# Key and value projection of a two-layer decoder: six slabs and eight plain quads per group, a new order of their jobs, squares by pairs of chunks

## The chip, the cores and the metric

The kernel runs on one core of a Trainium2 chip. The metric is device time in microseconds (us) of one execution of the whole program, as the median of several runs. All data are float32. Where the text says PE, DVE, ACT, POOL and SP it means TensorE, VectorE, ScalarE, GpSimd and SyncE.

## The reference, cut to what matters

Two layers work on a stream of 256 tokens of width 2048. Layer 0 is a pooling mixer beside a memory attention, then an MLP. From the stream after layer 0 the keys and values are made once. Layer 1 is a differential attention over them, a memory attention and an MLP. The change lies in `shared_kv` and around it:

```
def shared_kv(x, kv_norm, w_kv, k_norm, cos, sin):
    B, S, _ = x.shape
    kv = rms_norm(x, kv_norm) @ w_kv
    k1 = kv[..., :DIFF_QK_WIDTH].reshape(B, S, DIFF_HEADS, DIFF_HEAD_DIM)
    k2 = kv[..., DIFF_QK_WIDTH:2 * DIFF_QK_WIDTH].reshape(B, S, DIFF_HEADS, DIFF_HEAD_DIM)
    v = kv[..., 2 * DIFF_QK_WIDTH:].reshape(B, S, DIFF_HEADS, DIFF_V_DIM)
    k1 = partial_rope(rms_norm(k1, k_norm), cos, sin)
    k2 = partial_rope(rms_norm(k2, k_norm), cos, sin)
    return k1, k2, v
```

`w_kv` is 2048 x 3072: 768 columns of `k1`, 768 of `k2` and 1536 of `v`. The mean square of each token, which `rms_norm` needs, is applied after the product, as a factor per token.

## The kernel before, in words

**Three matmuls for one product.** Every weight is split into a part `hi`, rounded by an ACT cast (L195), and a part `lo`, the rest, by a DVE subtraction (L198). The activations are split in the same way. A product of 128 rows of weights is then three matmuls: low activations by `hi`, high by `hi`, high by `lo` (L1650 to L1652). The split weights stand in a ring of six slots of 512 columns (`hi_ring`, `lo_ring`). A job takes one or two neighbouring slots, a slot is free again when the job's matmuls are done, and `AHEAD` is three: splits of up to three later jobs are put into the program ahead of a job's matmuls. So for a slot the chain is: last matmul on it, cast, subtraction, next matmul.

**Quads and slabs.** The 3072 columns of `w_kv` are done as a last block of 512 columns of keys (tile `k1`), a last block of values (tile `v1`, the steps H), and two groups of 1024 columns, one of values (`vp`) and one of keys (`kp`). In a group the work comes in two shapes. A plain quad is one 128-row chunk of the stream by 512 columns, for both halves of the tokens: two products, six matmuls, one slot, loaded with another quad in one DMA of SP into a `raw` tile. A slab is two chunks by 1024 columns by the two halves of the tokens in seven products in place of eight: two by two blocks, with sums of blocks of the stream (`kv_sums`, made on DVE and ACT ahead) and sums of blocks of weights. Its job 0 is two products on one side of the weights and takes two slots, job 1 is one product and one slot, jobs 2 and 3 are two products and two slots each: 21 matmuls where four plain quads have 24. The sums of weights are made while the weights come in: the left half of a slab is loaded by SP (L158), job 0 splits it, then POOL adds the right half to it by an accumulating DMA (`add_right`, L170), and job 1 can be split only after that DMA has landed. In the same way POOL's second accumulating DMA stands between the splits of job 2 and of job 3. Two DVE additions per slab (L224, L238) make the other sums. Left halves stand in three buffers (tag `rows`), second ones in three (`feed.second`).

**The order of the jobs** is written by hand in the string `steps` (L1726): a pair of digits is a slab and its job (slabs 0 to 4 of values, 5 to 9 of keys), H a step of `v1`, A and B plain quads of values, C and D of keys, M a step of the memory values of layer 1 (tile `mv`), which the loop at L1870 makes, E and X, Y copies and closings. `close` (L1654) adds a group's seven banks up on DVE and ACT once the group's last slab is through. A scheduler then orders what the program says on each engine, so the queues differ a little from the program text.

**Other work of the same stretch** is hung on a counter that goes up with every step: `at(d, fn)` runs `fn` at the d-th step from now. Under way are the squares of the stream for its mean square (`later_square`, L752), the second load and split of the memory (`mem_again`, `mem_split`, tile `mems`), the sums of the stream's blocks (`kv_sums`, L1594), and at the end the normalisation of the keys and the scaled stream of layer 1 (`x_mx`). `two_squares` (L1334) exists already: it squares two chunks with one ACT instruction into the one buffer of tag `rowsq` and adds them on DVE to a sum of 512 columns; the last call adds the two halves.

Of the kernel before, what the change touches and what calls it, by code (L numbers as in the profile page):

```python
# [10 lines left out]
F32 = mybir.dt.float32  # L11
F32R = mybir.dt.float32r
AF = mybir.ActivationFunctionType
# [4 lines left out]
P = 128  # L18
T = 256
NK = 16  # L20
# [291 lines left out]
def program(ctx, tc, plan, dry, xT, memT, par, lam, cst, wst, yT):  # L312
    nc = tc.nc
# [3 lines left out]
    tp = ctx.enter_context(tc.tile_pool(name="tp", bufs=1))  # L317
# [5 lines left out]
    acc = {}  # L323
# [18 lines left out]
    def vt(name):  # L342
        return tp.tile([P, T], F32, tag="v", bufs=6, name=name)
# [13 lines left out]
    resid = cp.tile([P, NK, T], F32, name="resid")  # L357
# [40 lines left out]
    def gcol(c):  # L398
        return param[:, c : c + 1]
# [342 lines left out]
    def add_square(key, src, first):  # L742
# [5 lines left out]
        sq = vt("psq")  # L748
        nc.scalar.activation(sq, src, AF.Square)
        nc.vector.tensor_add(acc[key], acc[key], sq)  # L750

    def later_square(n):  # L752

        if n == 0:
            acc["x"] = tp.tile([P, T], F32, tag="acc", bufs=1, name="acc")
            nc.scalar.activation(acc["x"], resid[:, 0, :], AF.Square)
            return
        sq = vt("later")
        nc.scalar.activation(sq, resid[:, n, :], AF.Square)
        nc.vector.tensor_add(acc["x"], acc["x"], sq)  # L760

    def resid_add(ps, n):
        nc.vector.tensor_add(resid[:, n, :], resid[:, n, :], ps[:, 0:T])
# [784 lines left out]
    x_kv = sp.tile([P, NK, 512], F32R, tag="S2", name="x_kv")  # L1548
    x_in.append(x_kv)
    down()  # L1550
    for n in range(NK):
        at(2 + n // 2, lambda n=n: later_square(n))
    kv = sp.tile([P, 4096], F32, tag="big", name="kv1")
    kv2 = sp.tile([P, 2048], F32, tag="big2", name="vv1")
    kT = kv[:, 0:3072].rearrange("p (c t) -> p c t", c=12)
# [7 lines left out]
    def mem_again(p):  # L1563
        t = kv[:, p % 3 * 512 : p % 3 * 512 + 512].rearrange("p (k t) -> p k t", k=2)
        nc.sync.dma_start(t, memT[:, 2 * p : 2 * p + 2, :])

    def mem_split(k):
        t = kv[:, k % 6 * T : k % 6 * T + T]
        split_gain(mems1[:, k, :], t, gcol(G_MEM + 16 + k))

    for p in range(8):
        at(5 * p + 3 if p >= 3 else 4 + p // 2, lambda p=p: mem_again(p))
    for k in range(NK):
        at(12 + 9 * k // 4, lambda k=k: mem_split(k))

    ktab = rope_tables(G_KR, "krope")
    qtab = rope_tables(G_QR, "qrope")
# [16 lines left out]
    def kv_sums(i):  # L1594

        a = [vt("kv_a") for _ in range(2)]
        for e in range(2):
            k = 2 * i + e
            nc.scalar.activation(a[e], resid[:, k, :], AF.Copy, scale=gcol(G_KV + k))
        hi, lo = sums[:, i, 0:512], sums[:, i, 512:1024]  # L1600
        f = kv[:, 1536:2048]
        s1, s2, s3, s4 = (f[:, c * P : c * P + P] for c in range(4))
        (a11, a21), (a12, a22) = ((x[:, 0:P], x[:, P:T]) for x in a)
        if i >= 5:
            nc.vector.tensor_sub(s1, a11, a21)
            nc.vector.tensor_sub(s2, a12, a22)
            hi, lo, f = hi[:, 0:T], lo[:, 0:T], f[:, 0:T]
        else:
            nc.vector.tensor_sub(s1, a21, a22)
            nc.vector.tensor_sub(s3, a11, a21)  # L1610
            nc.vector.tensor_sub(s2, s1, a11)
            nc.vector.tensor_add(s4, a12, s2)

        def split():
            nc.scalar.copy(hi, f)
            nc.vector.tensor_sub(lo, f, hi.bitcast(F32))

        at(1, split)

    for i, d in enumerate((16, 23, 30, 38, 48, 42, 45, 52)):  # L1620
        at(d, lambda i=i: kv_sums(i))

    c1 = []
# [5 lines left out]
    def kv_groups():  # L1629
# [51 lines left out]
        slab = {}  # L1681

        def job(n, j):
            g, i = divmod(n, 5)
            if j == 0:
                slab[n] = feed.slab(
                    [blocks_of(g, 2 * i, c) + blocks_of(g, 2 * i + 1, c) for c in range(2)]
                )

            def plain(c, t):  # L1690
                x = x_kv[:, 2 * i + c, :]
                return x[:, t * P : t * P + P], x[:, T + t * P : T + t * P + P]

            def summed(c):
                return tuple(sums[:, i, b + c * P : b + c * P + P] for b in (0, 512))

            sides = (
                ((0, lambda: plain(0, 0)), (1, lambda: plain(1, 0))),
                ((2, lambda: summed(0)),),
                ((3, lambda: summed(1)), (4, lambda: summed(3))),  # L1700
                ((6, lambda: plain(1, 1)), (5, lambda: summed(2))),
            )
            hi, lo = feed.job(slab[n], j)
            for c, (p, a) in enumerate(sides[j]):
                s = slice(512 * c, 512 * c + 512)
                product(g, p, a(), hi[:, s], lo[:, s])
            feed.job_used(slab[n], j)
            tick()
            if i == 4:
                close(g, j)  # L1710

        def plain_quad(g, c, k):
            what = blocks_of(g, k, c)
            hi, lo = feed.quad(what if len(what) > 1 else what[0])
            x = [(x_kv[:, k, t * P : t * P + P], x_kv[:, k, T + t * P : T + t * P + P]) for t in range(2)]
            if c:
# [7 lines left out]
        last_v = []  # L1724
        ps = [pp.tile([P, 512], F32, tag=g, bufs=1, name="v1") for g in "ot"]
        steps = """  # L1726
            H H H H
            00 H H H H
            10 H 01 H 02 H H
            20 H 11 H H H E 12 30 03  # L1730
            A 21 A 22 A 13 A
            40 B 31 B 32 B 23 B
            B B 41 A 42 A 33 X 50
            C 43 C 60 C C 51 52
            D 70 C 61 62 C 53
            D 80 D 71 72 D 63
            90 D 81 D 82 Y 73 M M
            M 91 M 92 M 83 M
            M M 93
        """.split()  # L1740
        last_of = {}
        for n, x in enumerate(steps):
            if x in "ABCD":
                g, bs = dict(A=(0, (1, 6)), B=(0, (4, 2)), C=(1, (4, 2)), D=(1, (1, 6)))[x]
            elif x[0].isdigit():
                g, bs = int(x[0]) // 5, ((0, 1), (2,), (3, 4), (5, 6))[int(x[1])]
            else:
                continue
            for p in bs:
                last_of[g, p] = n  # L1750
        now_at = [-1]
        count = dict.fromkeys("HABCD", 0)
        values = dict(A=(0, 0), B=(0, 1), C=(1, 1), D=(1, 0))

        def more():

            while steps:
                x = steps.pop(0)
                now_at[0] += 1
                n = count.get(x, 0)  # L1760
                if x in count:
                    count[x] += 1
                if x == "M":
                    return True
                if x == "H":
                    wide_step(ps, ("w_kv", 0, n, 5, 4), x_kv, n)
                elif x == "E":
                    for t in range(2):
                        last_v.append(tp.tile([P, 512], F32, tag=("acc2", "rowsq")[t], bufs=1, name="v_c"))
                        nc.scalar.activation(last_v[t], ps[t], AF.Copy, scale=c1[0][:, t : t + 1])  # L1770
                elif x in "XY":
                    close("XY".index(x), 4)
                elif x in values:
                    plain_quad(*values[x], 10 + n)
                else:
                    job(int(x[0]), int(x[1]))
            return False

        def end():
# [364 lines left out]
```

## Time and profile before

| | |
|---|---|
| runs before | 1983.72, 1983.87, 1984.21 us, median 1983.87 us |
| the profiled execution | 1983.49 us |
| its span, first to last instruction | 1981.5 us |
| granted clock of PE | 1.00 throughout |
| PE, DVE, ACT busy share of the span | 100%, 91%, 79% |
| the stretch of the change | about 880 to 1110 us from the span's start: `k1` at 920 to 942, `v1` and `vp` to 1007, `kp` to 1055, then the rest of `mv` and the memory keys |

The profile is of one execution. Its own time is 2.0 us longer than its span and 0.38 us below the median of the runs. Busy time counts the stretches in which an engine has an instruction under way. Matmuls overlap each other, so a PE that is busy all the time is not yet shown to be free of waiting: there the starts of the matmuls have to be read.

### The profile page before, as it was taken

The numbers are of one execution on the slowest core, as the hardware profiler recorded it, in microseconds if no ns is written. First come the engines' busy times: TensorE is split into PE (matmuls) and PEld (weight loads), VectorE is DVE, ScalarE is ACT, GpSimd is POOL, SyncE is SP. The second block draws the span as 40 slices with busy tenths as digits, with TensorE's granted clock in tenths as the row PEclk, the third lists the DMA queues.
The fourth block names the chain that finished last, engine by engine and source line by source line (L and its number), as shares of the span: only waits on it lengthen the run. The fifth ranks groups of instructions, "written<-read, shape, count | busy, mean of one in ns | idle before, by whom it ended". The sixth has DMA issues, their size and how long they took to land.

```text
span 1981.5 us, 31968 instructions
## 1 busy us (share of the span) xinstructions
PE 1977.1 (100%) x10356; PEld 1685.5 (85%) x10356; DVE 1806.3 (91%) x3320; ACT 1569.6 (79%) x2894; POOL 238.7 (12%) x281
## 2 busy tenths in 40 slices
PE   9999999999999999999999999999999999999999
PEld 8888888888888888888888889888888888888888
DVE  8888889999999999889989798989999999999888
ACT  7766677788878888778868699777788888888775
POOL 0000011111111111110110000001111111111110
PEclk9999999999999999999999999999999999999999
DMA  9556578888888898766885534568888888888764
GB/s 316 181 184 198 187 203 233 237 228 235 237 232 233 228 235 227 226 183 228 244 223 191 162 126 145 195 188 242 234 230 230 234 234 228 242 231 231 229 203 146
DMA packets 151080, 426.92 MB, mean 215 GB/s; under 512 B 17024, under 2 KB 19712, under 8 KB 150912
## 3 DMA queue, kind: packets, MB, share of 16 engines
q1 hardware_dynamic: 111024, 352.50, 53.3%
q0 software_dynamic: 39744, 72.37, 21.9%
q8 instruction: 81, 1.33, 0.3%
q14 instruction: 87, 0.71, 0.1%
q10 hardware_dynamic: 144, 0.01, 0.0%
HBM read 422.72 MB, written 2.10 MB: 214 GB/s over the span
## 4 chain that ended last, share of the span: by engine, by line
PE 99%; DMA 0%; SPq 0%; ACT 0%; issue 0%; DVE 0%
PE x_bank L456 22%; PE x_bank L458 11%; PE p L953 10%; PE p L955 10%; PE p L956 10%; PE wo L456 6%; PE wo L458 3%; PE u L456 2%; PE ff L456 1%; PE u L458 1%; PE q L490 1%; PE q L492 1%; PE q L491 1%; PE mk L492 1%; PE mk L490 1%; PE mk L491 1%
## 5 line engine op out<-in xcount | busy, mean ns | idle before, releaser
L195 ACT CAST hi_ring<-raw 128x512 fp32r<-128x512 f32 x897 | 546.7, 619 | 169.4 <-PE x_bank L456 40.8
L198 DVE TENSOR_TENSOR lo_ring<-raw,hi_ring 128x512 fp32r<-128x512 f32 x897 | 605.2, 687 | 48.1 <-ACT hi_ring L195 42.0
L456 PE MATMUL x_bank<-fx,hi_ring 128*128 128x512 f32 x1728 | 540.1, 394 | 0.0
L458 PEld LDWEIGHTS x_bank<-fx,lo_ring 128*128 128x128 f32 x1728 | 324.5, 188 | 73.5
L198 DVE TENSOR_TENSOR lo_ring<-room,hi_ring 128x1024 fp32r<-128x1024 f32 x256 | 312.7, 1222 | 43.5 <-ACT hi_ring L195 41.7
L195 ACT CAST hi_ring<-room 128x1024 fp32r<-128x1024 f32 x256 | 269.4, 1052 | 96.2 <-PE x_bank L456 45.2
L458 PE MATMUL x_bank<-fx,lo_ring 128*128 128x256 f32 x1728 | 339.5, 278 | 0.0
L456 PEld LDWEIGHTS x_bank<-fx,hi_ring 128*128 128x128 f32 x1728 | 286.4, 189 | 26.0 <-ACT room L840 1.5
L198 DVE TENSOR_TENSOR lo_ring<-slab,hi_ring 128x1024 fp32r<-128x1024 f32 (+1 forms) x276 | 263.3, 954 | 33.8 <-ACT hi_ring L195 30.8
L195 ACT CAST hi_ring<-slab 128x1024 fp32r<-128x1024 f32 (+1 forms) x276 | 227.4, 834 | 53.9 <-PE p L955 28.5
L170 POOL DMA_DIRECT2D slab<-in_w x138 | 119.2, 864 | 1172.8 <-DVE lo_ring L198 1166.4
L953 PE MATMUL p<-hi_ring,sit 128*128 128x512 f32 x480 | 188.3, 392 | 0.0
L955 PE MATMUL p<-hi_ring,sit 128*128 128x512 f32 x480 | 187.5, 391 | 0.0
L956 PE MATMUL p<-lo_ring,sit 128*128 128x512 f32 x480 | 186.6, 389 | 0.0
L170 POOL DMA_DIRECT2D room<-in_w x128 | 110.5, 863 | 486.6 <-DVE lo_ring L198 457.2
L456 PE MATMUL wo<-cat,hi_ring 128*128 128x512 f32 x512 | 161.6, 397 | 0.0
L953 PE MATMUL p<-hi_ring,z 128*128 128x512 f32 x368 | 145.2, 394 | 0.0
L955 PE MATMUL p<-hi_ring,z 128*128 128x512 f32 x368 | 143.9, 391 | 0.0
L956 PE MATMUL p<-lo_ring,z 128*128 128x512 f32 x368 | 143.4, 390 | 0.0
L458 PEld LDWEIGHTS wo<-cat,lo_ring 128*128 128x128 f32 x512 | 95.9, 188 | 22.3
L956 PEld LDWEIGHTS p<-lo_ring,sit 128*128 128x128 f32 x480 | 90.1, 188 | 19.7
L953 PEld LDWEIGHTS p<-hi_ring,sit 128*128 128x128 f32 x480 | 90.0, 188 | 13.1
(498 smaller groups left out, 3613.6 us busy)
## 6 DMA issues: line engine op xcount, KB each, us to landing
raw<-in_w SPq DMA_DIRECT2D x446, 512.0 KB, 4.3
slab<-in_w SPq DMA_DIRECT2D x138, 512.0 KB, 5.7
slab<-in_w POOLq DMA_DIRECT2D x138, 256.0 KB, 5.4
room<-in_w SPq DMA_DIRECT2D x128, 256.0 KB, 4.7
room<-in_w POOLq DMA_DIRECT2D x128, 256.0 KB, 5.5
resid<-in_x SPq DMA_DIRECT2D x8, 256.0 KB, 5.0
kv<-in_mem SPq DMA_DIRECT2D x8, 256.0 KB, 4.2
out_y<-resid SPq DMA_DIRECT2D x16, 128.0 KB, 1.9
```

The costliest lines, as they stand in the source:

```text
L170: self.nc.gpsimd.dma_start(t, self.wst[h, :, 0:512], accum_op=ALU.add)
L195: self.last_cast = self.nc.scalar.copy(hi, src)
L198: low = self.nc.vector.tensor_sub(lo, src, hi.bitcast(F32))
L456: nc.tensor.matmul(ps, hi, xs[:, k, :], start=first and c == 0, stop=False)
L458: nc.tensor.matmul(ps[:, T : 2 * T], lo, xs[:, k, 0:T], start=False, stop=last and c == len(ks) - 1,)
L490: nc.tensor.matmul(ps[t], x[t][1], hi, start=k == 0, stop=False)
L491: nc.tensor.matmul(ps[t], x[t][0], hi, start=False, stop=False)
L492: nc.tensor.matmul(ps[t], x[t][0], lo, start=False, stop=k == NK - 1)
L953: nc.tensor.matmul(ps, a[1], hi, start=new, stop=False, **again)
L955: nc.tensor.matmul(ps, a[0], hi, start=False, stop=False, **again)
L956: nc.tensor.matmul(ps, a[0], lo, start=False, stop=end, **again)
```

## The change: what it does

In each of the two groups the sixth pair of chunks, which was four plain quads, becomes a sixth slab: slabs 0 to 5 are of values, 6 to b (eleven, in hexadecimal) of keys, and four chunks are left for the plain quads. The string of steps is written anew, with as many steps in all (16 H, 48 jobs and 16 plain quads, where there were 16 H, 40 jobs and 24 plain quads). The sixth pair's sums are made in the long form that a slab needs. The times of the memory's loads and splits and of the sums are moved, and the squares of the stream are made by `two_squares`, eight calls in place of sixteen of `later_square`.

```
-    for n in range(NK):
-        at(2 + n // 2, lambda n=n: later_square(n))
+    for n in range(8):
+        at(2 + n, lambda n=n: two_squares("x", resid, 2 * n))
...
-        at(5 * p + 3 if p >= 3 else 4 + p // 2, lambda p=p: mem_again(p))
+        at(5 * p + 2 if p >= 3 else 3 + p // 2, lambda p=p: mem_again(p))
-        at(12 + 9 * k // 4, lambda k=k: mem_split(k))
+        at(11 + 5 * k // 2, lambda k=k: mem_split(k))
...
-        if i >= 5:
+        if i >= 6:
...
-    for i, d in enumerate((16, 23, 30, 38, 48, 42, 45, 52)):
+    for i, d in enumerate((13, 19, 26, 33, 42, 50, 39, 46)):
...
-            g, i = divmod(n, 5)
+            g, i = divmod(n, 6)
-            if i == 4:
+            if i == 5:
...
-            B B 41 A 42 A 33 X 50
-            C 43 C 60 C C 51 52
-            D 70 C 61 62 C 53
+            A 51 A 52 43 X 60
+            C 53 C 70 61 62
+            C 80 71 D 72 63
...
-                    plain_quad(*values[x], 10 + n)
+                    plain_quad(*values[x], 12 + n)
```

DVE at the passage from values to keys, before. The rows L1669, L1668 and L1664 close banks of values (tile `vp`), `slab_9413` is the first slab of keys (5), and the 1024-column row on `vv` after L1664 splits the last job of values, 43:

```order
L198 TENSOR_TENSOR lo_ring<-vv_8728,hi_ring 128x1024
L1669 TENSOR_TENSOR kv_8727<-kv_8727,vp 128x512
L1668 TENSOR_TENSOR kv_8727<-kv_8727,vp 128x512
L198 TENSOR_TENSOR lo_ring<-slab_9413,hi_ring 128x1024
L1670 TENSOR_TENSOR kv_8727<-kv_8727 128x512
L198 TENSOR_TENSOR lo_ring<-raw_9380,hi_ring 128x512
L1664 TENSOR_TENSOR kv_8727<-kv_8727,vp 128x512
L198 TENSOR_TENSOR lo_ring<-vv_8728,hi_ring 128x1024
```

The same place of the changed program, whose lines stand ten lower (L1654 is what L1664 was). `slab_9385` is the first slab of keys (6), `slab_9431` the second (7), and `kv_8727` in a 1024-column row is the second buffer of slab 5, here for its job 53:

```order
L198 TENSOR_TENSOR lo_ring<-vv_8728,hi_ring 128x1024
L1654 TENSOR_TENSOR kv_8727<-kv_8727,vp 128x512
L1659 TENSOR_TENSOR kv_8727<-kv_8727,vp 128x512
L1658 TENSOR_TENSOR kv_8727<-kv_8727,vp 128x512
L198 TENSOR_TENSOR lo_ring<-slab_9385,hi_ring 128x1024
L1660 TENSOR_TENSOR kv_8727<-kv_8727 128x512
L198 TENSOR_TENSOR lo_ring<-raw_9356,hi_ring 128x512
L198 TENSOR_TENSOR lo_ring<-kv_8727,hi_ring 128x1024
L198 TENSOR_TENSOR lo_ring<-raw_9404,hi_ring 128x512
L198 TENSOR_TENSOR lo_ring<-slab_9431,hi_ring 128x1024
```

All three closings now stand ahead of the first split of keys, and that split, the last one of values and the next slab's follow each other with one plain quad between.

ACT during the pass over `k1`, before. `later` are squares of one chunk, each into a buffer of its own out of six:

```order
L759 ACTIVATE later<-resid 128x256 x3
L195 CAST hi_ring<-raw_8743 128x512
L759 ACTIVATE later<-resid 128x256 x2
L195 CAST hi_ring<-raw_8743 128x512
L759 ACTIVATE later<-resid 128x256 x2
```

And in the changed program, with `sq` for the squares of two chunks, all in one buffer:

```order
L1335 ACTIVATE sq_8805<-resid 128x512
L195 CAST hi_ring<-raw_8704 128x512
L195 CAST hi_ring<-raw_8743 128x512
L1605 CAST kv_sums<-kv_8727 128x512
L1335 ACTIVATE sq_8816<-resid 128x512
L195 CAST hi_ring<-raw_8743 128x512
L433 ACTIVATE mems_8729<-kv_8727,param 128x256
L195 CAST hi_ring<-raw_8768 128x512
L1335 ACTIVATE sq_8829<-resid 128x512
```

Between two squares there now stand two or three casts, each square waiting for the addition of the one before, and the first sums of the stream have moved up among them.

More of the change, by code (lines that the diff above doesn't have):

```diff
@@ L750, in add_square @@
         nc.vector.tensor_add(acc[key], acc[key], sq)
[L752 to L760, printed above, removed]
     def resid_add(ps, n):
@@ L1726, in kv_groups @@
         steps = """
-            H H H H
-            00 H H H H
+            H H H
+            00 H H H
             10 H 01 H 02 H H
-            20 H 11 H H H E 12 30 03
-            A 21 A 22 A 13 A
-            40 B 31 B 32 B 23 B
-            B B 41 A 42 A 33 X 50
-            C 43 C 60 C C 51 52
-            D 70 C 61 62 C 53
[L1736 to L1739, printed above, removed]
+            20 H 11 H 12 H
+            30 H H H E 21 22 03 13
+            A 40 A 31 B 32 23
+            B 50 B 41 B 42 33
+            A 51 A 52 43 X 60
+            C 53 C 70 61 62
+            C 80 71 D 72 63
+            C 90 81 D 82 73
+            D a0 91 92 83
+            b0 D a1 a2 Y 93 M M
+            M b1 M b2 M a3 M
+            M M b3
         """.split()
@@ L1744, in kv_groups @@
                 g, bs = dict(A=(0, (1, 6)), B=(0, (4, 2)), C=(1, (4, 2)), D=(1, (1, 6)))[x]
-            elif x[0].isdigit():
-                g, bs = int(x[0]) // 5, ((0, 1), (2,), (3, 4), (5, 6))[int(x[1])]
+            elif len(x) == 2:
+                g, bs = int(x[0], 16) // 6, ((0, 1), (2,), (3, 4), (5, 6))[int(x[1])]
             else:
@@ L1773, in more @@
                 elif x in values:
-                    plain_quad(*values[x], 10 + n)
+                    plain_quad(*values[x], 12 + n)
                 else:
-                    job(int(x[0]), int(x[1]))
+                    job(int(x[0], 16), int(x[1]))
             return False
```

## The prediction

> **What bounds the kernel now.** I read the page first, its span, engines and chain:
>
> ```profile
> span 1981.5 us, 31968 instructions
> PE 1977.1 (100%) x10356; PEld 1685.5 (85%) x10356; DVE 1806.3 (91%) x3320; ACT 1569.6 (79%) x2894; POOL 238.7 (12%) x281
> PE 99%; DMA 0%; SPq 0%; ACT 0%; issue 0%; DVE 0%
> ```
>
> The third row is the page's chain that ended last in short: it never leaves PE. So time goes only if PE gets fewer matmuls, or waits less. Next, the busy time by stretch (us, then busy us and count of PE, PEld, DVE, ACT and POOL, granted clock, DMA share, GB/s) where the edits lie:
>
> ```profile
> 913.00:948.00 35.00, 35.00 (x173) 29.53 (x171) 32.65 (x77) 31.09 (x71) 0.86 (x1) 1.00 0.64 215
> 948.00:985.00 37.00, 37.00 (x165) 30.61 (x164) 36.57 (x68) 29.45 (x51) 6.04 (x7) 1.00 0.85 237
> 985.00:1055.00 70.00, 70.00 (x311) 57.90 (x310) 61.11 (x81) 48.00 (x70) 10.35 (x12) 1.00 0.78 216
> 1055.00:1080.00 25.00, 25.00 (x118) 20.69 (x117) 25.00 (x64) 23.20 (x51) 0.00 (x0) 1.00 0.56 190
> ```
>
> The clock is full throughout. DVE idles 2.35 us in the first stretch, 0.43 in the second, 8.89 in the third, 11.67 us in all, and not at all in the fourth. Then PE's timeline (start, length, what) of 33 matmuls in a row around the passage from values to keys:
>
> ```profile
> 996.66 0.39 PE L1650 MATMUL vp<-hi_ring,kv_sums 128*128 128x512 f32 x1
> ...
> 1003.23 0.39 PE L1652 MATMUL kp<-lo_ring,x_kv 128*128 128x512 f32 x1
> ...
> 1003.91 0.39 PE L1652 MATMUL kp<-lo_ring,kv_sums 128*128 128x512 f32 x1
> ```
>
> 32 steps in 7.25 us: a matmul every 0.2266 us, though each is 0.39 us long. All 33 stand in this even rhythm, so here PE waits for nothing. The price of a matmul is 0.2266 us, not 0.39.
>
> **The change part by part.** *Matmuls.* Four plain quads are 24 matmuls, a slab 21. In each of two groups one slab takes the place of four quads: 6 fewer, at 0.2266 us a gain of **1.36 us**. By the length in the rows, 0.39 us, it would be 2.3 us. The Trainium skill, page "TensorE: Matmul & The Clock Gate", section "Back-to-back issue gap", gives about 131 ns for a matmul of 512 columns in a sustained stream and 216 ns for an isolated one; by these the gain would be 0.8 or 1.3 us. The trace's 226.6 ns decides against the 131.
>
> *DVE's work.* Its rows before, by shape (count | busy us, mean ns | idle before):
>
> ```profile
> L198 DVE TENSOR_TENSOR lo_ring<-slab,hi_ring 128x1024 fp32r<-128x1024 f32 x10 | 12.2, 1222 | 1.6 <-ACT hi_ring L195 1.5
> L198 DVE TENSOR_TENSOR lo_ring<-slab,hi_ring 128x512 fp32r<-128x512 f32 x10 | 6.9, 686 | 0.0
> L760 DVE TENSOR_TENSOR acc<-acc,later 128x256 f32<-128x256 f32 x10 | 4.2, 416 | 0.0
> L1610 DVE TENSOR_TENSOR kv<-kv_a 128x128 f32<-128x128 f32 x5 | 1.4, 284 | 0.0
> ```
>
> and its timeline at the passage:
>
> ```profile
> 998.40 1.22 DVE L198 TENSOR_TENSOR lo_ring<-vv,hi_ring 128x1024 fp32r<-128x1024 f32 x1 [0.97 <-ACT hi_ring L195]
> 999.58 0.69 DVE L1669 TENSOR_TENSOR kv<-kv,vp 128x512 f32<-128x512 f32 x1
> 1000.33 0.69 DVE L1668 TENSOR_TENSOR kv<-kv,vp 128x512 f32<-128x512 f32 x1
> 1000.93 1.22 DVE L198 TENSOR_TENSOR lo_ring<-slab,hi_ring 128x1024 fp32r<-128x1024 f32 x1
> 1002.07 0.68 DVE L1670 TENSOR_TENSOR kv<-kv 128x512 f32<-128x512 f32 x1
> 1002.67 0.69 DVE L198 TENSOR_TENSOR lo_ring<-raw,hi_ring 128x512 fp32r<-128x512 f32 x1
> ```
>
> Back to back the next starts 0.085 us before the last one ends (1000.93 to 1002.07 to 1002.67), so I take that off each length: 1.14 us for 1024 columns, 0.60 for 512, 0.33 for 256, 0.20 for 128. A slab is three 1024-column splits, one of 512 and two additions of 512: 5.2 us of DVE beside 21 x 0.2266 = 4.76 us of PE. Four quads were 2.4. Two slabs more: +5.6 us. Longer sums of the sixth pair: two subtractions of 128 and a split of 512 for one of 256, +0.7. Squares: 15 additions of 256 (5.0) become 7 of 512 and one of 256 (4.5), -0.5. Together **+5.8 us**, against 11.67 us idle, of which 1.36 go with PE's shorter time. That leaves 4.5 us: it fits on average, but where DVE was full PE will wait in places. In 948:985 DVE had only 0.43 us idle, and the new order puts slabs closer together there; what helps is that less is left to do before (squares, memory splits later). I put 0.0 to 0.9 us on this stretch.
>
> *ACT.* Its casts and squares (same columns):
>
> ```profile
> L195 ACT CAST hi_ring<-slab 128x1024 fp32r<-128x1024 f32 x10 | 10.5, 1046 | 4.1 <-PE kp L1651 3.6 <-PE vp L1651 0.5
> L195 ACT CAST hi_ring<-slab 128x512 fp32r<-128x512 f32 x10 | 6.2, 619 | 2.6 <-DMA slab<-in_w 1.9 <-PE vp L1651 0.6
> L759 ACT ACTIVATE later<-resid 128x256 f32<-128x256 f32 x10 | 3.7, 408 | 0.0
> ```
>
> Six more casts of 1024 and six fewer of 512: at most 6.3 - 3.7 = +2.6 us; 16 squares of 256 (at most 6.5) become 8 of 512, which I price like a cast of that size (5.0), -1.5. About +1 us, under PE: by the stretches above ACT idled 3.9, 7.5 and 22 us. The one buffer of the squares makes each wait for DVE's addition of the one before, and the casts behind it wait too. Cover: during `k1` each slot holds one quad, five other quads (5 x 6 x 0.2266 = 6.8 us) run between two uses of a slot, and cast and split take 0.62 + 0.69 of it. I take 0, with 0.6 us above (one 512-column addition awaited) and nothing below: PE kept its rhythm before.
>
> *The passage from values to keys.* The first keys' split waits on DVE behind L1668, which waits for bank 4 of the values. Before, that split started at 1000.93, was done at 1002.15, and PE used it at 1003.23: 1.08 us to spare, with a plain quad A (six matmuls) between the job that fills bank 4 and the end of values. The new steps, "52 43 X 60", have none there: 1.36 us less. 1.08 - 1.36 = -0.28: **0.3 us** of waiting at 60, unless PE's order covers it with high matmuls of the next job.
>
> *The accumulating DMAs.* From the page, what POOL issues for slabs (size, median us to landing); from the slab's tile between 935 and 1056 us, POOL's time for an issue (least, median, most) and the landings of SP's and POOL's transfers together:
>
> ```profile
> slab<-in_w POOLq DMA_DIRECT2D x138, 256.0 KB, 5.4
> ...
> L170 POOL DMA_DIRECT2D slab<-in_w x10: 862/862/865, 947.0 to 1031.9; - x10
> DMA to landing us min/median/max: 3.6/6.0/8.4
> ```
>
> Twice ACT stood for such a DMA (POOL's timeline, then ACT's):
>
> ```profile
> 1015.56 0.86 POOL L170 DMA_DIRECT2D slab<-in_w  x1 [1.95 <-DVE lo_ring L198]
> 1023.08 0.86 POOL L170 DMA_DIRECT2D slab<-in_w  x1 [2.74 <-DVE lo_ring L198]
> ...
> 1024.10 0.62 ACT L195 CAST hi_ring<-slab 128x512 fp32r<-128x512 f32 x1 [1.68 <-DMA slab<-in_w]
> 1030.57 0.62 ACT L195 CAST hi_ring<-slab 128x512 fp32r<-128x512 f32 x1 [0.25 <-DMA slab<-in_w]
> ```
>
> Those came 8.5 and 7.5 us after the issue. The split ahead of the second issue, on DVE's timeline:
>
> ```profile
> 1021.56 1.22 DVE L198 TENSOR_TENSOR lo_ring<-slab,hi_ring 128x1024 fp32r<-128x1024 f32 x1
> ```
>
> From the end of the split of job 0 (or 2) to the low part of job 1 (or 3) it takes 0.3 us to the issue (end at 1022.78, issue at 1023.08), the landing L, then cast and split: L + 1.6 with 512 columns (0.62 + 0.69), L + 2.6 with 1024 (1.05 + 1.22). Counted in steps of three matmuls (0.68 us), the shortest way from a job 0 to its job 1 was 14 (9.5 us); now 60 to 61 has 10 (6.8) and 70 to 71 has 9 (6.1). From a job 2 to its job 3 the shortest was 42 to 43 with 10; now 52 to 53 has 8 (5.4). To each come about 1 us by which the first split is ahead of its use (1.08 at the passage) and 0.45 until the third matmul asks for the low part. With L = 5.4, 71 has 7.0 of 7.5 us and is in time; 53 has 8.0 of 6.9 and is 1.1 us late, of which high matmuls of the next step cover up to 0.45. I take **0.7 us** in all; the ends are 0 (L of 4) and 4 us (L of 8.4).
>
> *Moved loads.* The memory's loads go one step earlier in SP's queue, past weight loads; before, ACT waited 1.8 us for them in all and PE's rhythm did not show it. Nothing on the path.
>
> The sum: -1.36 + 0.3 + 0.7 = -0.4 us, with the ends 0 and 0.9 of the full stretch left to the range. The profiled execution had 1983.49, so 1983.1; it lay 0.38 below the median, so **1983.5 us** for a median. With 0.3 to 2.2 us given back it is 1982.8 to 1984.7.
>
> **The rivals.** *All is covered.* The banks close in time, the DMAs land in 4 us: 1983.87 - 1.36 = 1982.5 us, and 1982.1 if 0.4 us of present waits goes too. For it: the even rhythm with DVE at 99% in 948:985. Against it: the three short distances.
>
> *The DMAs come late.* L of 7.5 to 8.4 at two of the three places costs 3 to 5 us: 1985.5 to 1987.5. For it: four more such DMAs in the same time. Against it: once PE has waited at 53, 61 and 71 have that time too.
>
> *DVE becomes the bound; slower.* Most of DVE's idle time between 913 and 1056 us is no free time (waiter, whom for, us in total, times, longest):
>
> ```profile
> DVE lo_ring L198 <- ACT hi_ring L195: 10.4, 17, 1.4
> ...
> ACT hi_ring L195 <- PE kp L1651: 10.2, 9, 2.1
> ACT hi_ring L195 <- PE vp L1651: 9.0, 10, 1.4
> ```
>
> DVE waits for casts, which wait until PE has freed a slot. Five slab jobs now have only 9 matmuls (2.04 us) between the freeing of their slots and their first use, where the least was 12 (2.72), and cast and split take 1.05 + 1.22. If the ring's hand-over, not DVE's free time, decides from there on, each added DVE microsecond lengthens the stretch: 5.8 - 1.36 = +4.4 us, 1988.3 us. The point is where a run of slabs leaves no idle time ahead of it to be used; between 985 and 1055 there were 8.89 us, which speaks against it.
>
> *POOL is kept from its issues.* The Trainium skill, page "SBUF — State Buffer", section "Who interferes with whom", says that a DMA issued by POOL stalls when DVE holds the port pair that the two share, since POOL then cannot write the descriptors; of operations with two inputs in SBUF, which DVE's splits are, it takes it (as inferred) that they leave that free. A busier DVE would then hold back the four added DMAs, and the three short ways. Its price by rows: one 1024-column split of 1.22 us at each, 3.7 us in all, 1983.5 + 3.7 = 1987.2. Against it: an issue took 0.862 to 0.865 us in all ten cases, with DVE 92% busy (130.3 of 142 us from 913 to 1055). By that rule there should be scatter; the trace shows none.
>
> *It gains much.* More than 4 us would need waits of PE to vanish that the rhythm does not show.
>
> That six matmuls go is certain from PE's order: per group 116 with high and 58 with low weights, where 118 and 59 were.
>
> **How the numbers follow.** A measurement of this kernel can tell about 0.2%, 4 us, from no change: faster is below 1979.9, slower above 1987.8. Chances: the forecast 0.59, all covered 0.17, late DMAs 0.13, DVE as the bound 0.07, POOL kept off 0.02, much gained 0.02. Slower is DVE as the bound and the upper ends of the two DMA cases, 0.09; faster 0.02; same 0.89. The range runs from 1982.1, the floor of the covered case, to 1986.8, most of the way through late DMAs; it leaves out DVE as the bound, the rest of the late DMAs, much gained and the edge of the covered case, under 0.2.
>
> **What would show it.** Right: 116 + 58 rows per group in `vp` and `kp`; starts 0.2266 us apart but for gaps of under 1 us at 60 and 53; DVE near full from 948 to 1040. Wrong: gaps of over 1 us at 61, 71 or 53 behind a DMA (late DMAs); many small gaps before 1024-column jobs with DVE above 98% through the stretch (DVE as the bound); POOL issues above 1 us; no gap at all (covered). Wrong altogether would be a change of time outside 880 to 1110 us.

## The result, and the profile after

The changed kernel takes 1995.3 us (median of 6 runs, 1993.0 to 1996.63), the kernel before 1984.04 us (6 runs): a ratio of 1.0056 with a 95% interval of 1.0043 to 1.0069. It is 11 us slower; 1983.5 was forecast, with a range from 1982.1 to 1986.8. The profiled execution took 1994.93 us. Its page, in the same three rows as before:

```profile
span 1993.2 us, 31944 instructions
PE 1980.8 (99%) x10350; PEld 1682.3 (84%) x10350; DVE 1812.3 (91%) x3319; ACT 1571.5 (79%) x2886; POOL 242.2 (12%) x285
...
PE 95%; issue 2%; DVE 1%; DMA 1%; ACT 0%; POOL 0%; SPq 0%; POOLq 0%; ACTq 0%; DVEq 0%
```

PE still carries the chain, but 4 to 5% of it now goes through other engines and DMAs. The two middle stretches of the busy time by stretch, with the columns as before:

```profile
948.00:985.00 37.00, 35.16 (x152) 27.82 (x151) 33.12 (x59) 26.44 (x44) 6.04 (x7) 1.00 0.67 189
985.00:1055.00 70.00, 64.92 (x269) 48.95 (x268) 58.67 (x74) 41.41 (x57) 12.94 (x15) 1.00 0.81 214
```

In these 107 us the rows count 421 matmuls of PE, before 476 (one that reaches over an edge counts on both sides). The 55 missing ones at 0.2266 us are 12.5 us of waiting, where there was practically none. Less the six saved matmuls (1.36 us) that is 11.1 us, nearly all of the 11.44 us between the two profiled executions. The clock is full. DVE is *less* busy than before, 91.8 us in place of 97.7: it waits too. So over the stretch no engine became full; things became late. Who waited for a DMA in 948 to 1056 us (waiter, whom for, us in total, times, longest):

```profile
ACT hi_ring L195 <- DMA slab<-in_w: 11.2, 5, 3.4
...
ACT hi_ring L195 <- DMA kv<-in_w: 4.1, 1, 4.1
...
ACT hi_ring L195 <- DMA raw<-in_w: 2.4, 2, 2.3
```

ACT's casts stand 17.7 us for weights; before, the two waits that the prediction shows were 1.9 us. Four of these waits, with POOL's issues on its timeline and then ACT's casts:

```profile
991.35 0.86 POOL L170 DMA_DIRECT2D slab<-in_w  x1 [3.85 <-DVE lo_ring L198]
...
1004.03 0.86 POOL L170 DMA_DIRECT2D kv<-in_w  x1 [7.21 <-DVE lo_ring L198]
...
1021.07 0.86 POOL L170 DMA_DIRECT2D slab<-in_w  x1 [2.08 <-DVE lo_ring L198]
...
1035.43 0.86 POOL L170 DMA_DIRECT2D slab<-in_w  x1 [2.61 <-DVE lo_ring L198]
```

```profile
998.79 0.62 ACT L195 CAST hi_ring<-slab 128x512 fp32r<-128x512 f32 x1 [2.87 <-DMA slab<-in_w]
...
1010.26 1.05 ACT L195 CAST hi_ring<-kv 128x1024 fp32r<-128x1024 f32 x1 [4.07 <-DMA kv<-in_w]
...
1028.31 0.62 ACT L195 CAST hi_ring<-slab 128x512 fp32r<-128x512 f32 x1 [3.39 <-DMA slab<-in_w]
...
1044.54 0.62 ACT L195 CAST hi_ring<-slab 128x512 fp32r<-128x512 f32 x1 [3.18 <-DMA slab<-in_w]
```

These are jobs 51, 53, 81 and a1. From issue to cast it is 7.4, 6.2, 7.2 and 9.1 us, where the forecast took 5.4. ACT works its queue in order, so every cast behind the waiting one is late as well. PE at job 51 and at the passage from values to keys shows what that does (in brackets the idle time and what ended it):

```profile
999.99 0.50 PE L1640 MATMUL vp<-hi_ring,x_kv 128*128 128x512 f32 x1 [0.85 <-ACT hi_ring L195]
...
1007.38 0.39 PE L1641 MATMUL kp<-hi_ring,x_kv 128*128 128x512 f32 x1
1008.58 0.73 PE L1642 MATMUL kp<-lo_ring,x_kv 128*128 128x512 f32 x2 [0.81 <-DVE lo_ring L198]
...
1010.36 0.39 PE L1642 MATMUL kp<-lo_ring,x_kv 128*128 128x512 f32 x1
1011.36 0.50 PE L1640 MATMUL vp<-hi_ring,x_kv 128*128 128x512 f32 x1 [0.61 <-ACT hi_ring L195]
1011.70 0.40 PE L1641 MATMUL vp<-hi_ring,x_kv 128*128 128x512 f32 x1
1012.62 0.50 PE L1642 MATMUL vp<-lo_ring,x_kv 128*128 128x512 f32 x1 [0.53 <-DVE lo_ring L198]
```

The first row is not of job 51, which takes sums of the stream (`kv_sums`), but of a plain quad (`x_kv`) whose cast stands behind 51's. 1007.38 to 1008.58 is 1.20 us, 0.98 more than the rhythm: job 60. 1010.36 to 1011.36 and 1011.70 to 1012.62 are 0.77 and 0.70 us more: job 53, whose high and low parts come late. Taken so from all starts of matmuls, the places are:

| place (us) | jobs | PE waits, us | what was last |
|---|---|---|---|
| 966 to 970 | 12, 30 | 1.6 | a quad's load of SP (2.3 us of ACT), then DVE's queue |
| 977 to 980 | 03, 13 | 1.3 | ACT's queue, behind the sums of the stream |
| 999 to 1001 | 51 | 1.4 | landing |
| 1006 to 1008 | 43, 60 | 1.2 | DVE's closings, themselves late since 51 (see e2) |
| 1010 to 1013 | 53 | 1.7 | landing |
| 1028 to 1030 | 81 | 0.7 | landing |
| 1038 to 1042 | 92, 83, b0 | 1.2 | DVE and ACT, late since 81 |
| 1044 to 1049 | a1, a2, 93 | 2.9 | landing |

Taken together these transfers were not slower than before: between 945 and 1056 us they took 5.5 us to land on average in both kernels (20 issues before, 23 after), and 7 us or more in 4 cases before and in 6 after. What changed is where the long ones fall, and how little room there is. SP's queue has a part in both. What SP waited for between 935 and 1056 us, before (L156 loads quads, L158 left halves of slabs, L160 second ones):

```profile
SPq L156 <- DVE lo_ring L198: 44.6, 16, 5.2
SPq L158 <- DVE vv L238: 22.5, 5, 6.6
SPq L158 <- DVE kv L238: 7.1, 1, 7.1
```

and after:

```profile
SPq L158 <- DVE vv L238: 32.6, 5, 8.6
SPq L160 <- DVE lo_ring L198: 23.1, 6, 10.6
SPq L156 <- DVE lo_ring L198: 15.4, 5, 9.1
SPq L158 <- DVE kv L238: 10.8, 2, 5.7
SPq L158 <- DMA slab<-in_w: 10.7, 5, 7.0
```

Before, SP mostly stood at a quad's load. After, it stands at a slab's load, until L238 frees one of the three buffers. The loads stand in the order of use, so those of the quads behind it wait too, and then go in a bunch. Counting loads that start less than 1.2 us apart as one bunch, between 935 and 1056 us, 6 bunches of 29 had three or more loads before, and 9 of 18 after. SP's timeline ahead of the longest landing:

```profile
1033.47 0.33 SPq L158 DMA_DIRECT2D slab<-in_w  x1
1033.85 0.48 SPq L156 DMA_DIRECT2D raw<-in_w  x1
1034.45 0.36 SPq L160 DMA_DIRECT2D vv<-in_w  x1
1034.85 0.44 SPq L156 DMA_DIRECT2D raw<-in_w  x1
```

Four loads, 1.8 MB, went out in 1.4 us, and POOL's 256 KB came half a microsecond later. The DMA issues from 1035.4 to 1036 us, and for comparison one of POOL's from 1018.1 to 1018.5 us, with no other load under way (KB, us to landing):

```profile
slab<-in_w POOLq DMA_DIRECT2D x1, 256.0 KB, 9.1
...
vv<-in_w POOLq DMA_DIRECT2D x1, 256.0 KB, 3.7
```

The transfer for 53 is not such a case: no load was under way at its issue at 1004.03 us, and it took 6.1 us. Three loads of SP, 1.3 MB, went out 0.5 to 2.2 us behind it.

### The profile page after: what moved, and what is told of

Read it like the earlier page. It is cut to its first block, busy times and chain, and to the rows that moved or that the text cites. A ratio compares the mean times of both kernels' runs of the same rounds, so it can differ in the third digit from the quotient of the medians.

```text
span 1993.2 us, 31944 instructions
## 1 busy us (share of the span) xinstructions
PE 1980.8 (99%) x10350; PEld 1682.3 (84%) x10350; DVE 1812.3 (91%) x3319; ACT 1571.5 (79%) x2886; POOL 242.2 (12%) x285
## 4 chain that ended last, share of the span: by engine, by line
PE 95%; issue 2%; DVE 1%; DMA 1%; ACT 0%; POOL 0%; SPq 0%; POOLq 0%; ACTq 0%; DVEq 0%
PE x_bank L456 22%; PE x_bank L458 11%; PE p L943 10%; PE p L945 10%; PE p L946 10%; PE wo L456 6%; PE wo L458 3%; PE u L456 2%; PE ff L456 1%; PE u L458 1%; PE q L490 1%; PE q L492 1%; PE q L491 1%; PE mk L492 1%; PE mk L490 1%
```

## The experiments

All times are medians, beside a kernel before of 1983.85 to 1984.11 us on the same chip. "Gaps" is what the starts of the matmuls between 948 and 1055 us have beyond the rhythm of 0.2266 us, in the profiled execution: 0.1 us before, 12.5 in the changed kernel.

| run | time, us | ratio to before (95%) | gaps, us |
|---|---|---|---|
| e1 squares alone | 1984.18 | 1.0000 (0.9991 to 1.0009) | 0.6 |
| e2 after, no accumulating DMAs | 1986.10 | 1.0009 (1.0000 to 1.0018) | 4.3 |
| e3 before, no accumulating DMAs | 1984.06 | 0.9999 (0.9990 to 1.0009) | 0.3 |
| e4 six slabs for values alone | 1994.93 | 1.0055 (1.0041 to 1.0069) | 10.6 |
| e5 after, old times | 1994.66 | 1.0054 (1.0040 to 1.0068) | 12.7 |
| e6 after, longer ways from slab 4 on | 1991.77 | 1.0037 (1.0023 to 1.0051) | 10.1 |
| e7 after, wide order | 1989.29 | 1.0029 (1.0017 to 1.0041) | 5.5 |
| e8 after, loads out of turn | 1989.38 | 1.0026 (1.0017 to 1.0036) | 5.8 |
| e9 e7 and e8 together | 1986.78 | 1.0017 (1.0008 to 1.0026) | 6.4 |
| e10 before, loads out of turn | 1983.79 | 1.0000 (0.9990 to 1.0009) | 0.1 |
| e11 e6 and e8 together | 1987.98 | 1.0021 (1.0012 to 1.0030) | 5.7 |
| e12 after, three loads ahead | 1996.49 | 1.0063 (1.0048 to 1.0078) | 15.4 |
| e13 as e9, wider | 1987.00 | 1.0016 (1.0007 to 1.0025) | 3.6 |
| e14 e13 without accumulating DMAs | 1984.91 | 1.0006 (0.9996 to 1.0015) | 2.1 |

Theory: POOL's transfers land too late, and since SP's loads come in bunches. Rival: DVE's added work is the bound.

**e1, the squares alone.** The kernel before, with this edit:

```
-    for n in range(NK):
-        at(2 + n // 2, lambda n=n: later_square(n))
+    for n in range(8):
+        at(2 + n, lambda n=n: two_squares("x", resid, 2 * n))
```

> The kernel before with one edit of the change alone: the squares of the stream by pairs of chunks. Theory (the 12.5 us of PE waiting in the changed kernel come from the slabs: transfers that land late and queues that stand behind them): no gap of PE over 0.1 us between 948 and 1055 us, time within 1 us of before. Rival (the one buffer of the squares makes ACT's casts wait, and what is late at 966 to 970 us in the changed kernel stems from it): gaps of 1 to 2 us in all there, 1.5 us slower.

1984.18 us, and no gap over 0.18 us. The one buffer of the squares costs nothing that can be measured.

**e2 and e3, no accumulating DMAs**, in the changed kernel and in the one before:

```
     def add_right(self, n, t):
+        if self.in_turn:
+            return
```

> The changed kernel without POOL's accumulating DMAs in the key and value groups: it leaves out the sums of the two halves of the weights, so that the splits of jobs 1 and 3 and the addition after job 1 no longer wait for a landing, and 24 x 256 KB less are moved; the matmuls, casts, splits and additions are as many as in the changed kernel. Theory (late landings cause most): the gaps at jobs 51, 53, 81, a1 and what follows them (7.9 us of the 12.5) go, the time falls to 1987 us or below; what was late for DVE's queue at 12, 30, 03 and 60 stays, about 4 us. Rival (DVE's work is the bound): nothing of DVE's is taken away, so the time stays above 1992 us.

> The kernel before without the same DMAs (the sums of halves of weights are left out in both groups). Control for the run of the changed kernel without them. Both theories: PE waited for none of them before, so the time stays within 1 us of 1984. A fall of more than 1 us would say that part of what the changed kernel gains without them has nothing to do with the change.

1986.1 us: 9.2 of the 11.3 us go, and the kernel before does not move. DVE has the same work as in the changed kernel. Its second stretch:

```profile
985.00:1055.00 70.00, 70.00 (x306) 56.83 (x305) 65.94 (x86) 49.54 (x69) 0.00 (x0) 1.00 0.52 175
```

Behind 985 us PE's gaps fall from 9.4 to 0.9 us, with DVE busier (65.94 us) than in the changed kernel (58.67): DVE's amount of work is not the bound there. The wait at 60, which was expected to stay, went too. Ahead of 985 us 3.4 us of gaps stay, as expected. The run takes away the wait and 6 MB of traffic together, so it does not tell which of the two it was.

**e4, six slabs for values alone**: the values' order of the changed kernel, then keys in five slabs (6 to a) and twelve plain quads:

```
-            C 53 C 70 61 62
-            C 80 71 D 72 63
...
+            C 53 C 70 C C 61 62
+            D 80 C 71 72 C 63
+            D 90 D 81 82 D 73
...
```

> Six slabs for values as in the changed kernel, five slabs and twelve plain quads for keys in nearly the order of before; four plain quads of keys take sums of the stream in the form made for a slab, which differ from theirs. Three matmuls fewer than before (-0.7 us). Theory (each wait belongs to a place of the order: a short way or a full queue there): the gaps at 12, 30, 03, 51, 60 and 53 stay, 7.2 us, and none over 0.5 us follow after 1015 us: 1990.5 us. Rival (the total of DVE's work decides, wherever it is put): half of the added work, half of the loss, spread also over the keys: 1988 to 1990 us with gaps of 2 us or more after 1015 us.

1994.93 us: neither theory said so much. The values cost 6.7 us of the 7.2 expected, but the keys, which have five slabs again, another 3.9. There ACT stood at a quad, not at a slab:

```profile
1036.73 0.62 ACT L195 CAST hi_ring<-raw 128x512 fp32r<-128x512 f32 x1 [3.64 <-DMA raw<-in_w]
```

This quad's load was among the last of four, 1.8 MB, that SP issued from 1026.27 to 1028.66 us, behind a slab's load. That pointed at SP's bunches, more than at the number of slabs. What followed on PE is told in the last section.

**e5, old times** for the memory and, as far as their uses allow, for the sums:

```
-        at(11 + 5 * k // 2, lambda k=k: mem_split(k))
+        at(12 + 9 * k // 4, lambda k=k: mem_split(k))
...
-    for i, d in enumerate((13, 19, 26, 33, 42, 50, 39, 46)):
+    for i, d in enumerate((16, 23, 30, 38, 45, 52, 42, 48)):
```

> The changed kernel with the memory's loads and splits at the times of before and the sums of the stream as late as their uses allow (16, 23, 30, 38, 45, 52, 42, 48). Theory (what PE waits between 957 and 981 us, jobs 12, 30 and 03, comes from this moved work, which stands in DVE's and ACT's queues ahead of the splits; what follows comes from landings): 2.9 us of gaps there fall below 1.5, those behind 985 us stay within 1.5 us of 9: about 1993.5 us. Rival (slabs that lie closer are enough to fill DVE there): the gaps at 957 to 981 us stay above 2.5 us.

1994.66 us, and the gaps between 948 and 985 us are 4.1 us, in the changed kernel 3.1: the theory fell here. The moved work is not what makes jobs 12, 30 and 03 late.

**e6, longer ways from slab 4 on**, and **e7, a wide order from the start** (with the times of before and the sums at 16, 23, 30, 38, 44, 51, 47, 53). Of e6, from slab 4 on:

```
-            A 40 A 31 B 32 23
-            B 50 B 41 B 42 33
-            A 51 A 52 43 X 60
-            C 53 C 70 61 62
+            A 40 A 31 A 32 23
+            A 50 B 41 X B 42 33
+            B 60 B 51 52 43
+            C 70 C 61 62 53
...
```

> The changed kernel with another order of the jobs from slab 4 on and nothing else: as many jobs and matmuls of each kind, but at least 15 steps of three matmuls from job 0 to job 1 and 13 from job 2 to job 3 for slabs 4 to 8 (the changed kernel: 17, 13, 10, 9, 13 and 11, 8, 11, 13, 11), and the closing of the values' second bank five jobs ahead of the keys. Theory (short ways leave a landing no time): the gaps at 51, 43/60, 53 and 81 go (5.0 us) and what follows them shrinks, 3 us stay at 12, 30 and 03 and up to 2 at a1: 1985.5 to 1988 us. Rival (DVE's total work): the same work, so 1993 us or more.

> Six slabs and four plain quads per group as in the changed kernel, in an order that begins as the kernel before does and has at least 13 steps from job 0 to job 1 and 11 from job 2 to job 3 for every slab, with the memory's work at the times of before and the sums spread out. Theory (ways and places, not the amount of work): no gap over 0.6 us but perhaps one or two behind 1030 us, 2 us in all at most, six matmuls fewer: 1982.5 to 1985 us. Rival (the added work of DVE has no room): 1988 us or more.

In e6 the gaps at 51, 60, 53 and 81 are gone, as the short ways would have it. But the one at 965 us grew to 2.0 us (ACT stood 3.6 us for a quad), and new ones came, of 1.1 us at 1019 and of 2.1 us at 1040 us (a landing); the first and the last have a stretch of half the clock behind them. e7 has 0.3 us of gaps from 948 to 1006 us and 5.2 behind. Both were off their forecasts by 4 us, and e7 is within its rival's range: longer ways alone do not do it.

**e8, loads out of turn**, and **e10**, the same in the kernel before:

```
-        feed.in_turn = True
+        feed.in_turn = False
```

> The changed kernel with SP's loads of the groups left to the scheduler's order instead of the order of use, so that a quad's load no longer stands behind a slab's load that waits for its buffer. Theory: ACT no longer waits 2.3 us for a quad at 963 us and the gaps at 12 and 30 (1.6 us) shrink by half or more; the accumulating DMAs are as late as before or later, since a slab's load comes later: 1990 to 1996 us. Rival (loads in the order of use are not what holds ACT at 963 us): the gaps at 12 and 30 stay as they are.

> The kernel before with SP's loads of the groups out of turn and nothing else: a control. Theory: before, SP waited for slab buffers with time to spare and PE for no load, so the time stays within 1 us of 1984. A fall would say that what e8 gained has nothing to do with the change.

The scheduler now puts quads' loads ahead of a slab's load that would stand. 1989.38 us, 5.9 us less; before does not move. The gaps at 12, 30, 51, 81 and a1 are gone, though jobs, DMAs and DVE's work are the same. What SP waited for at slabs:

```profile
SPq L158 <- DVE vv L238: 13.0, 6, 6.1
SPq L158 <- DVE kv L238: 7.6, 3, 4.1
```

That is 20.6 us, where the rows on L238 and on the slab alone were 54.1, and 3 bunches of 30 have three loads, none more. The transfers for 51, 53, 81 and a1 now take 6.3, 5.8, 5.8 and 5.6 us; how much of the gain is theirs and how much comes from quads that are in time, this run does not tell. The gaps at 60 and 53 stay (1.0 and 1.2 us): ACT still stands 1.7 us for 51's transfer and 3.5 us for 53's, since the order leaves them too little time.

**e12, three loads ahead** in place of four (`feed.loads_ahead = 3`):

> The changed kernel, loads in the order of use, with loads put into the program for three loads ahead of a split in place of four, so that a slab's load comes later and stands less long ahead of the quads' loads for its buffer. Theory (bunches behind a waiting slab load): fewer bytes ahead of POOL's transfers, the gaps at 51, 81 and a1 (5 us) fall by half or more: 1988 to 1992 us. Rival (the landings need an earlier issue): later loads, longer waits, 1995 us or more.

1996.49 us, as the rival had it. But SP stood 55.4 us at slabs' loads (54.1 in the changed kernel) and still sent four loads, 1.8 MB, in a bunch at 1035 us. So the bunches were not smaller, and the run says nothing on what smaller ones would do.

**e9 and e11, both remedies together**:

> The wide order of the jobs (the run e7) with SP's loads out of turn. Theory (what is left in e7 are landings behind bunches that SP releases after a wait for a slab's buffer): the gaps behind 1005 us, 4.4 us in e7, fall below 1.5 us: 1983 to 1985 us. Rival (DVE and the ring have no room in the keys): they stay above 3 us, 1987 us or more.

> The order with long ways from slab 4 on (the run e6) with SP's loads out of turn. Theory: the two waits for landings in e6 at 965 and 1040 us, each with a stretch of half the granted clock behind it (5.8 us and 6.5 us in all), go with the bunches; left are about 1 us at 03 and 1 to 2 us elsewhere: 1984.5 to 1987 us. Rival (the landings are late for another reason than SP's order): above 1989 us.

1986.78 and 1987.98 us. The remedies add in part: each alone took 6 us (or 3.5, e6), both 8.5 (or 7.3). e11 is a little above its forecast's end; e9 lies between theory and rival. Its profiled execution is its slowest (1989.84 us, 1.5 us of it half the clock), and the 6.0 us of gaps behind 1005 us in it are the rival's.

**e13 and e14**, e9 with longer ways from job 2 to job 3, and the same without accumulating DMAs:

```
-            B 41 X B 42 33 60
+            B 41 X 42 B 33 60
...
-            C 81 D 82 73 a0
+            C 81 82 D 73 a0
...
```

> As e9 (wide order, loads out of turn), with the order mended once more: at least 13 steps from job 2 to job 3 for slabs 1 to a (e9: 11 at slabs 4, 8 and 9), the keys' second bank closed ahead of the last plain jobs. Theory (what e9 still waits are landings where the way from job 2 to 3 is 11): of e9's gaps the 1.5 us at 83 goes, the closing's 0.4 us at 1009 stays: 1984 to 1986 us, still not under 1983. Rival (six slabs in this stretch leave DVE and ACT no room, wherever the jobs stand): 1986.5 us or more.

> The same as e13 without POOL's accumulating DMAs in the groups (the sums of the two halves of the weights are left out, 24 x 256 KB less are moved). Theory (all that is left are landings, and DVE and ACT have room for the added work): 1982.5 to 1983.5 us, 1.4 us less matmuls and gaps of 0.5 us or less in all. Rival (DVE's or ACT's queue still costs something in this order): gaps of over 1 us stay and the time is 1984 us or more.

e13 gains nothing on e9: the rival's 1986.5 us or more. e14 takes 1984.91 us: 2.1 us of e13's time went with the landings (each median is good to 1.8 us, so this is near the edge of what the runs tell apart), and 2.1 us of gaps stay in which no DMA has a part, as the rival had it. The largest, 0.8 us at 1019.5 us, has DVE busy without a break ahead of it (the lines stand two lower in this kernel; L1664 to L1666 close the last banks of values):

```profile
1014.88 0.68 DVE L1664 TENSOR_TENSOR kv<-kv,vp 128x512 f32<-128x512 f32 x1
1015.47 0.68 DVE L200 TENSOR_TENSOR lo_ring<-slab,hi_ring 128x512 fp32r<-128x512 f32 x1
1016.08 0.68 DVE L1665 TENSOR_TENSOR kv<-kv 128x512 f32<-128x512 f32 x1
1016.68 0.68 DVE L200 TENSOR_TENSOR lo_ring<-raw,hi_ring 128x512 fp32r<-128x512 f32 x1
1017.28 0.67 DVE L1666 TENSOR_TENSOR kv<-kv,vp 128x512 f32<-128x512 f32 x1
1017.88 2.35 DVE L200 TENSOR_TENSOR lo_ring<-vv,hi_ring 128x1024 fp32r<-128x1024 f32 x2
```

What ended PE's wait there was a cast of ACT, which had itself stood for a slot of the ring until PE freed it:

```profile
1019.46 1.05 ACT L197 CAST hi_ring<-slab 128x1024 fp32r<-128x1024 f32 x1 [2.34 <-PE kp L1643]
```

So here the rival has a part: DVE is full for a moment where the closings fall among close slabs, and the ring leaves ACT no slot. Which of the two decides is not shown. No version with six slabs came below the kernel before; whether one can is open.

## Why the prediction was wrong, point by point

- **Six matmuls fewer:** right. `vp` and `kp` have 116 + 58 rows each; 1.36 us stands in every sum above.
- **The amounts of DVE and ACT:** right. DVE's busy time grew by 6.0 us (5.8 was worked out), ACT's by 1.9 (1). Squares and moved loads at nothing: right (e1, and e5 within its interval).
- **The passage, 0.3 us at 60:** the place was right, the size was 1.0 us (1.2 with 43). The three closings stand back to back ahead of the split, as the order showed:

```profile
1004.38 1.22 DVE L198 TENSOR_TENSOR lo_ring<-vv,hi_ring 128x1024 fp32r<-128x1024 f32 x1
1005.51 0.68 DVE L1654 TENSOR_TENSOR kv<-kv,vp 128x512 f32<-128x512 f32 x1
1006.11 0.68 DVE L1659 TENSOR_TENSOR kv<-kv,vp 128x512 f32<-128x512 f32 x1
1006.71 0.68 DVE L1658 TENSOR_TENSOR kv<-kv,vp 128x512 f32<-128x512 f32 x1
1007.31 1.22 DVE L198 TENSOR_TENSOR lo_ring<-slab,hi_ring 128x1024 fp32r<-128x1024 f32 x1
```

  But the first of them stands behind the split of 43, which PE itself had to wait for after 51 had landed late. The 1.08 us to spare were read from a kernel in which nothing was late. Without the accumulating DMAs (e2) the same three closings stand ahead of the split, and PE's gap there is under 0.1 us. So the closings alone cost next to nothing, and the 1.0 us belongs with the landings.
- **The accumulating DMAs, 0.7 us: this step failed.** It took every landing at 5.4 us, the median of before, though single ones already took up to 8.4, and it priced three ways alone, to 61, 71 and 53. 61 and 71 were in time, as forecast. 53 cost 1.7 us. 51 and 81 with 13 steps and a1 with 11, which are also shorter than the 14 of before and were not looked at, cost another 5.0: their landings took 7 to 9 us. The room was put too high as well. By the prediction's count 13 steps give 8.8 us and the lead and the third matmul 1.45 more, so 81 with its landing of 7.2 us would need 8.8 of 10.3 and be in time. But the split of job 80 ended at 1020.78 us, and PE, had it not waited, would have asked for 81's low part at 1029.1: 8.3 us. And at 51 the sum had no place for a quad whose cast stands behind the late one. With what came late behind 81, landings make 7.9 of the 12.5 us by the table, and with 60 about 9; without them 4.3 stay (e2).
- **What the sum left out:** SP's queue. "Moved loads. Nothing on the path" priced the memory's loads and no other. Two slabs more in three buffers make SP stand at each slab's load, and with the loads in the order of use all that is behind it. That is 5.9 us (e8), half of the loss, which no rival had. It made quads late, and three of the four landings that cost most were shorter without it, by 1.1 to 3.5 us; that bunches ahead of a transfer lengthen it is argued from such cases, not shown by a run of its own.
- **The full stretch, 948 to 985 us, 0 to 0.9 us:** 3.1 us by the starts. It was not filled by DVE, which was busy 33.1 us there (before 36.6). With loads out of turn the gaps there fall to 1.1 us (e8), with the early order and the times of before to nothing (e7), without the accumulating DMAs they stay (3.4, e2).
- **The rivals.** The late DMAs named the mechanism, and their sign, a gap of over 1 us at 53 behind a DMA, came (1.7 in two parts); their price was made for two of three places, the waits were at four, and fed each other. "Against it: once PE has waited at 53, 61 and 71 have that time too" held for those two and not for 81 and a1. DVE as the bound gave 1988.3 us for a reason that the trace denies, DVE idling more than before; e14 leaves it, with the ring, up to 2 us at single places. POOL was not kept off: its issues still take 0.862 to 0.865 us, now beside twelve slabs.

From 1995.3 us down: loads out of turn -5.9 (e8), the wide order -2.4 (e13), landings -2.1 (e14), and about 2 us of DVE's and ACT's queues above the 1982.7 us that six matmuls fewer would give. The share of a step depends on the order in which they are taken: landings taken away first are 9.2 us (e2).

## What to carry to other kernels

When a change puts more into a fixed set of buffers, look first at the queue that issues the loads: a load that stands for its buffer holds back all behind it, and then lets them go in a bunch, beside transfers of other queues. A median landing time says little on a single transfer: here they ran from 3.7 to 8.4 us before and to 9.1 after, with the same mean, and the change put long ones on short ways. And a kernel whose bound engine never waits says little on its slack; the leads of each step have to be read one by one, the smallest first.

## What the hardware showed that was not expected

**Half the clock after short waits.** In e4 PE waited 1.4 and 0.7 us within 3 us (rows: start, length, and the wait in brackets), and then ran at half speed:

```profile
1036.71 0.39 PE L1642 MATMUL kp<-lo_ring,x_kv 128*128 128x512 f32 x1
1038.34 0.50 PE L1640 MATMUL kp<-hi_ring,x_kv 128*128 128x512 f32 x1 [1.24 <-ACT hi_ring L195]
...
1039.60 0.50 PE L1642 MATMUL kp<-lo_ring,x_kv 128*128 128x512 f32 x1 [0.53 <-DVE lo_ring L198]
...
1040.32 0.63 PE L1641 MATMUL kp<-hi_ring,kv_sums 128*128 128x512 f32 x1
1040.74 0.63 PE L1642 MATMUL kp<-lo_ring,kv_sums 128*128 128x512 f32 x1
```

```profile
1040.00:1043.20 3.20, 3.20 (x9) 2.53 (x8) 3.09 (x5) 1.41 (x4) 0.86 (x1) 0.50 0.73 224
```

The granted clock is 0.50 in this stretch, with a matmul every 0.43 us; in all it lasts from 1039.98 to 1043.39 us, 3.4 us, and costs 1.6 us on top of 2.1 us of waiting. The same came twice in e6 and once each in e9 and e12, for 3.4 us each time. In the changed kernel's profile, where 2.9 us of waits lie in 5 us, it did not come, though two of its six runs list a mean clock of 0.999, as the runs with such a stretch do. The Trainium skill, page "TensorE: Matmul & The Clock Gate", section "What's actually happening", tells of half the clock after an idle window of about 3.4 us, with windows that run freely. The half speed and the length of 3.4 us agree; in e4 waits that add up to 2.1 us, the longer one of 1.4, were enough.

**Landing by what is under way.** A 256 KB transfer of POOL took 3.7 us with nothing else under way at its issue and 9.1 us half a microsecond behind 1.8 MB of SP's loads. Over the changed kernel's issues between 945 and 1056 us the time rises by about 1.7 us for each MB of SP's loads that is under way at the issue, over those before by as much (lines fitted to issues and landings); where loads go out of turn the tie is loose (0.5 in e10, 1.4 in e8), and with nothing under way the times still ran from 3.7 to 6.1 us. The Trainium skill, page "DMA: Bandwidth & Descriptors", section "Queues, rings and completion order", says that each DMA engine takes turns between the queues by packet; by that rule alone, with packets of like size, 256 KB from POOL would be delayed by about as many bytes of SP's (an estimate), 1.2 us at the 214 GB/s of the profile's page. The 5.4 us between the two transfers are more; why stays open.
